# The first two units project 400 tokens before their RMS norms are known, and the norms are multiplied into the results

## The chip, the cores and the metric

The kernel runs on one core of one Trainium2 chip. The time is that of the device, in microseconds (us), from start to end of one execution. The core's engines are TensorE (PE, matrix products into PSUM), VectorE (DVE), ScalarE (ACT), GpSimd (POOL) and SyncE (SP, which issues most DMAs); each works through its own instructions in order.

## The reference, cut to what matters

One encoder layer on two inputs of 256 and 2048 tokens of width 1024, with 16 learned tokens put ahead of each. `w_in` has 2816 columns: attention (q, k, v and a gate) and a convolution part (value, gate, output gate).

```python
def rmsnorm(x, w):
    y = xf * lax.rsqrt(jnp.mean(xf * xf, axis=-1, keepdims=True) + NORM_EPS)
    return y * w
...
    h = rmsnorm(z, norm_w)
    proj = jnp.einsum('bld,de->ble', h, w_in)
    q, k, v, g_att, c_val, c_glu, g_conv = jnp.split(proj, SPLIT_IDX, axis=-1)
...
    u = c_val * jax.nn.sigmoid(c_glu)       # then a convolution of width 31, LayerNorm, SiLU
...
    return z + jnp.einsum('ble,ed->bld', mixed, w_out)
```

The norm of a token is one factor for all of its 1024 values. So `h @ w_in` is the same as `(z * norm_w) @ w_in` times that factor per token.

## The kernel before

All products are made in float32 from two halves: a rounded high half and the low half that is left (`xh` and `xl` of an activation, in groups of up to 400 tokens; `ws` of a weight, both halves in one tile). A product is three matmuls for each 128 rows of depth, in the order (weight high, activation high), (weight high, activation low), (weight low, activation high): `PASSES`. The 1024 rows of depth are 8 steps, so that one half of a unit on one group is 24 matmuls, and an item (unit, group) is 48.

**Units and groups.** A unit is 256 columns of `w_in`: for the first units 128 gate and 128 value columns of the convolution part. The 2320 tokens are in six groups, g0 of 400 columns and g1 to g5 of 384. The order of items begins (unit 0, g0), (unit 1, g0), (unit 0, g1), (unit 1, g1), (unit 0, g2), (unit 1, g2), which are items 0 to 5; item 6 is (unit 2, g0). For an item of the convolution part, `c_group` makes the gate half (`pg`), takes its sigmoid on ACT (`sg`), makes the value half (`pv`), and multiplies both on DVE into `us`, from which DVE later makes the convolution in 30 taps and a first step per tile (L850 and L841).

**What a group needs.** `Prep` prepares a group in steps: `load` brings the transposed tokens in four tiles `xt` (each 2 steps of depth); `first` broadcasts the norms over the partitions by matmuls into `bc` (L661); `scale` multiplies `xt` by weight and norm on DVE (L681); `split` makes `xh` on ACT (L698) and `xl` on DVE and POOL in turn (L707). The norms come from `stats`: the tokens are loaded a second time, with a token in each partition (`xn`, 18 tiles of 128 and one of 16), squared and summed on ACT (L632) and raised to -1/2 on POOL (L122, L123).

**What a unit needs.** `weights` loads a unit in four quarters `wraw` of 256 KB, makes the high half on ACT (L742) and the low half on POOL or DVE (L743).

**The head.** In program order: SP loads `xn0` to `xn3`, `vec` (the norm weight and small vectors), `xt` 0 and 1 of g0, the quarters of unit 0, `xt` 2 and 3, `cw` (the taps), `xn4` to `xn6`, unit 1, then g1. No matmul of a projection starts before the squares of `xn0` to `xn3`, their rstd, the broadcast and the first scale. A scheduler orders the rest; work for later items is put into lists (`later`) that it serves between matmuls (`tick`). After the projections and convolutions, some 560 us in, comes LayerNorm, then attention and the output projection.

Of the kernel before, what the change touches and what calls it, by code (L numbers as in the profile page):

```python
# [75 lines left out]
def hymba_kernel(  # L76
# [56 lines left out]
    def owe(ns):  # L133
        credit[0] -= ns
# [483 lines left out]
    if True:  # L618
# [20 lines left out]
        class Prep:  # L639
# [6 lines left out]
            def load(self, d2):  # L646
# [5 lines left out]
                )  # L652

            def first(self):
                g, n = self.g, self.n
                bc = psum.tile([P, 512], F32, tag="c", name=f"bc{g}")
                segs = [(0, NM, 0)] if g == 0 else []
                for b in range(3 * g, 3 * g + 3):
                    segs.append((blk_local(b)[1], P, b + 1))
                for o, rows, i in segs:  # L660
                    nc.tensor.matmul(  # L661
                        bc[:, o : o + rows],
                        rstd[:rows, i : i + 1].to_broadcast([rows, P]),
                        ident[:rows, :rows],
                        start=True,
                        stop=True,
                    )
                if self.pool:
                    self.bc = sp.tile([P, 400], F32, tag="bcs", name=f"bcs{g}", bufs=1)
                    nc.scalar.copy(self.bc[:, :n], bc[:, :n])  # L670
                else:
                    self.bc = bc

            def scale(self, d2):
# [37 lines left out]
        def weights(k):  # L712

            key = keys[k]
            raw = {}

            def load(eng):
                pool = wl if k % 2 else wr
                ws = pool.tile([P, ND, 2, UW], F32R, tag="ws", name=f"ws{key[0]}_{key[1]}")
                wsplit[key] = ws  # L720
                if key[0] == 1 and key[1] >= CACHE:
                    for q in range(4):
                        part = ws[:, 2 * q : 2 * q + 2].rearrange("p d a n -> p (d a n)")
                        eng.dma_start(part.bitcast(F32), wd[key[1], q])
                    return
                for q in range(4):
                    if k == 1:
                        if q % 2 == 0:
                            pair = cp.tile([P, UWID], F32, tag="us", name=f"wraw{k}_{q}")
                        raw[q] = pair[:, 512 * (q % 2) : 512 * (q % 2) + 512].rearrange("p (a n) -> p a n", n=UW)  # L730
                    else:
                        raw[q] = sp.tile([P, 2, UW], F32, tag="wraw", name=f"wraw{k}_{q}", bufs=4)
                    dma = eng.dma_start(raw[q], w_in[key[1], :, 2 * q : 2 * q + 2, :])
                    if PIN_W <= k < 4:
                        tc.keep_in_program_order(dma)

# [10 lines left out]

            return load, split

# [10 lines left out]
        def proj_et(ws, half_i, g, o=0):  # L760
# [4 lines left out]
            for d in range(ND):  # L765
                for wi, xi in PASSES:
# [39 lines left out]
        def c_group(c, j, ws, g):  # L806
            n = GROUPS[g][1]
            pg = proj_et(ws, 0, g)
            sg = sp.tile([P, 400], F32, tag="sg", name=f"sg{c}_{j}_{g}")
            nc.scalar.activation(sg[:, :n], pg[:, :n], AF.Sigmoid)  # L810
            tick(24 * (n / 2.4 + 3))
            pv = proj_et(ws, 1, g)
            if g == 0:
# [181 lines left out]
        preps[0].load(2)  # L995
        preps[0].load(3)
        nc.sync.dma_start(cw, conv_w)
        nc.vector.scalar_tensor_tensor(kscale, vec[:, 20:21], -(HD ** -0.5), vec[:, 21:22], op0=ALU.mult, op1=ALU.mult)
        for i in (0, 1, 2, 3):
            r[i]()  # L1000
        preps[0].first()
        preps[0].alloc()
        preps[0].scale(0)
        for q in range(4):
            if q < 3:
                preps[0].scale(q + 1)
            preps[0].split(q)
            w01[0][1](q, nc.gpsimd if q % 2 else nc.vector)
        r = {i: stats(i) for i in (4, 5, 6)}
        w01[1][0](nc.sync)  # L1010

        def at_item_start(i, c, u, g):
            if i == 0:
                r[4]()
                r[5]()
                for q in range(4):
                    preps[1].load(q)
                    w01[1][1](q, nc.gpsimd if q % 2 else nc.vector)
                r[6]()
            if i == 1:  # L1020
                later(1, preps[1].first)
                later(1, preps[1].alloc)
                later(1, lambda: preps[1].scale(0))
                for q in range(4):
                    if q < 3:
                        later(1, lambda q=q: preps[1].scale(q + 1))
                    later(1, lambda q=q: preps[1].split(q))
                for k in range(7, 10):
                    later(1, lambda k=k: later(1, stats(k)))
                for q in range(4):  # L1030
                    later(2, lambda q=q: preps[2].load(q))
            if i == I2:
                later(1, preps[2].first)
                later(1, preps[2].alloc)
                later(1, lambda: preps[2].scale(0))
                for q in range(4):
                    if q < 3:
                        later(1, lambda q=q: preps[2].scale(q + 1))
                    later(1, lambda q=q: preps[2].split(q))

# [6 lines left out]

        for i, (c, u, g) in enumerate(items):
            if (c, u) == keys[-1] and g == CHUNKS[c][0]:
                while conv_q[0] or conv_q[1]:  # L1050
# [27 lines left out]
            for k in loads.get(i, []):  # L1078
                load, split = weights(k)
                load(nc.sync)  # L1080
# [85 lines left out]
```

## Time and profile before

| | us |
|---|---|
| time, median of 3 runs | 978.19 |
| the three runs | 978.15, 978.19, 2411.97 |
| the profiled execution, own time | 974.79 |
| its span in the profile | 973.0 |
| PE busy in it | 949.2 (98%), 5740 records |
| DVE busy | 755.9 (78%) |
| ACT busy | 424.6 (44%) |
| POOL busy | 341.2 (35%) |

The span runs from the first to the last instruction of the engines; all times in rows are from its start. Busy shares of several engines overlap. The median is of executions without a profile, so an estimate that is made in the trace has to be carried over by the difference of the two.

### The profile page before, as it was taken

To read this page: it belongs to the slowest core of one execution; us is meant where nothing else is said; L and a number is where in the kernel's file an instruction comes from. 1 tells how busy PE (TensorE), PEld (TensorE's weight loads), DVE (VectorE), ACT (ScalarE), POOL (GpSimd) and SP (SyncE) were. 2 spreads that over 40 slices of the span, in tenths; PEclk is the share of its full clock that TensorE was granted. 3 is DMA by queue.
4 is the path that set the end of the run, shared out by engine and by line. 5 is a ranking of instruction groups with operands and counts; after the bars stand their busy time and mean duration, and the time that the engine had idled before them with its cause. 6 is when DMAs were issued, how large, how long until landed. Compare 5 with 4: busy or idle time off the path is not lost.

```text
span 973.0 us, 16234 instructions
## 1 busy us (share of the span) xinstructions
PE 949.2 (98%) x5740; PEld 890.0 (91%) x5740; DVE 755.9 (78%) x1261; ACT 424.6 (44%) x1156; POOL 341.2 (35%) x541
## 2 busy tenths in 40 slices
PE   5999999999999999999999998899999999999998
PEld 5999999999999999999999998678888888888886
DVE  4759999998987699999993555877776777767772
ACT  6621111343468710111113454766665666666651
POOL 5500000364468300000002464745445544544451
PEclk9999999999999999999999998999999999999999
DMA  9643345785735222233335657954554445544321
GB/s 332 221 181 118 130 170 179 264 286 182 225 124 180 92 73 76 86 128 136 127 135 173 212 141 219 294 171 134 159 177 148 125 152 166 178 127 135 109 88 43
DMA packets 113872, 155.75 MB, mean 160 GB/s; under 512 B 10592, under 2 KB 77296, under 8 KB 113792
## 3 DMA queue, kind: packets, MB, share of 16 engines
q1 hardware_dynamic: 113648, 154.11, 48.1%
q0 software_dynamic: 144, 0.62, 0.4%
q8 instruction: 45, 0.74, 0.3%
q14 instruction: 35, 0.29, 0.1%
HBM read 101.00 MB, written 54.31 MB: 160 GB/s over the span
## 4 chain that ended last, share of the span: by engine, by line
PE 91%; DMA 3%; DVE 2%; POOL 1%; issue 1%; SPq 1%; ACT 0%; POOLq 0%; DVEq 0%
PE pj L767 42%; PE y L538 20%; PE pj L783 13%; PE O L464 5%; PE pT L429 4%; PE S L316 4%; DMA woraw<-in_w_out 2%; DMA snk<-in_sink 1%; DMA wraw<-in_w_in 1%; PE O L316 1%; PE lnt L183 1%; PE qT L316 1%; PE lnu L202 1%; PE kt L941 0%; PE pT_m L426 0%
## 5 line engine op out<-in xcount | busy, mean ns | idle before, releaser
L767 PE MATMUL pj<-xh,ws 128*128 128x384 f32 (+1 forms) x1536 | 397.2, 339 | 2.5 <-ACT xh L698 2.5
L850 DVE SCALAR_TENSOR_TENSOR y<-us,cw,y 128x1167 f32<-128x1167 f32 x240 | 329.0, 1428 | 0.6
L767 PEld LDWEIGHTS pj<-xh,ws 128*128 128x128 f32 x1536 | 282.3, 189 | 2.8 <-ACT xh L698 2.8
L767 PE MATMUL pj<-xl,ws 128*128 128x384 f32 (+1 forms) x768 | 262.5, 342 | 0.1
L783 PE MATMUL pj<-ws,xh 128*128 128x256 f32 (+1 forms) x880 | 165.8, 286 | 0.0
L767 PEld LDWEIGHTS pj<-xl,ws 128*128 128x128 f32 x768 | 144.7, 188 | 1.1 <-POOL xl L707 0.7
L783 PEld LDWEIGHTS pj<-ws,xh 128*128 128x128 f32 (+1 forms) x880 | 137.8, 189 | 0.3
L783 PE MATMUL pj<-ws,xl 128*128 128x256 f32 (+1 forms) x440 | 125.4, 285 | 0.0
L383 ACT ACTIVATE sb<-sb,nm 128x304 f32<-128x304 f32 (+4 forms) x144 | 77.1, 535 | 45.3 <-DVE nm L371 43.7
L538 PE MATMUL y<-wo,mch 128*128 128x512 f32 x288 | 95.9, 414 | 0.0
L538 PE MATMUL y<-wo,mah 128*128 128x512 f32 x288 | 93.7, 406 | 0.0
L441 DVE TENSOR_TENSOR pl<-pT,ph 128x512 fp32r<-128x512 f32 x100 | 69.0, 690 | 29.0 <-ACT ph L440 28.5
L875 ACT ACTIVATE go<-pj 128x384 f32<-128x384 f32 x48 | 23.6, 491 | 154.5 <-PE pj L767 145.3
L371 DVE CUSTOM_DVE_ANT_0 sb<-S,bias,nsnk 128x304 f32<-128x304 f32 (+4 forms) x144 | 73.5, 511 | 15.0 <-PE S L316 14.5
L783 PEld LDWEIGHTS pj<-ws,xl 128*128 128x128 f32 (+1 forms) x440 | 83.2, 189 | 0.2
L122 POOL TENSOR_SCALAR ssk<-ssk 128x2 f32<-128x2 f32 x18 | 6.4, 356 | 213.0 <-ACT sqk L889 212.9
L440 ACT CAST ph<-pT 128x512 fp32r<-128x512 f32 x100 | 58.2, 583 | 40.2 <-PE pT L429 39.5
L406 POOL TENSOR_SCALAR sb<-sb,es 128x304 f32<-128x304 f32 (+4 forms) x144 | 72.8, 525 | 3.6
L316 PEld LDWEIGHTS S<-kw,q 128*128 128x128 f32 x288 | 53.8, 191 | 17.9 <-DVE nm L371 5.9
L122 POOL TENSOR_SCALAR ssq<-ssq 128x4 f32<-128x4 f32 (+2 forms) x55 | 28.3, 515 | 114.4 <-ACT xn L632 76.9
L316 PE MATMUL S<-kw,q 128*128 128x304 f32 (+4 forms) x288 | 62.6, 299 | 5.3 <-DVE nm L371 5.3
L429 PE MATMUL pT<-ident,sb 128*128 128x128 f32 x400 | 61.6, 274 | 1.3 <-POOL sb L406 1.0
(118 smaller groups left out, 1441.8 us busy)
## 6 DMA issues: line engine op xcount, KB each, us to landing
wd<-ws SPq DMA_DIRECT2D x36, 512.0 KB, 5.7
ws<-wd SPq DMA_DIRECT2D x36, 512.0 KB, 5.3
wraw<-in_w_in SPq DMA_DIRECT2D x52, 256.0 KB, 5.6
xn<-in_z SPq DMA_DIRECT2D x18, 512.0 KB, 5.7
gd<-go SPq DMA_DIRECT2D x48, 192.0 KB, 2.1
yo<-in_z SPq DMA_DIRECT2D x36, 256.0 KB, 2.6
out_y<-yo SPq DMA_DIRECT2D x36, 256.0 KB, 2.4
kw<-kd SPq DMA_DIRECT2D x16, 512.0 KB, 5.7
```

Source lines behind the costliest of these rows:

```text
L316: r = f(*a, **k)
L371: nc.vector.tensor_tensor_reduce(out=sb[:, n, c0:c1], in0=ps[:, 0:w], in1=cst["bias"][:, kv, n, c0 - QB * n : c1 - QB * n], scale=1.0, sca ...
L383: nc.scalar.activation(sb[:, n, c0:c1], sb[:, n, c0:c1], AF.Exp, bias=nm[:, n : n + 1], scale=-1.0, accum_out=rs[:, n : n + 1],)
L406: nc.gpsimd.tensor_scalar(sb[:, k, a0:a1], sb[:, k, a0:a1], es[:, k : k + 1], 1.0, op0=ALU.mult, op1=ALU.mult)
L429: nc.tensor.transpose(pt[:, hl, :], sbt[b, kv][:, hl, KCOL[k] : KCOL[k] + P], ident)
L440: nc.scalar.copy(ph, pt)
L441: nc.vector.tensor_tensor(pl, pt, ph, op=ALU.subtract)
L464: nc.tensor.matmul(o, lhs, t, start=(start and i == 0), stop=(stop and i == 1))
L538: nc.tensor.matmul(ps, mh[mi][:, e % 4, :], wo[e, wi][:, cols], start=(e == 4 and k == 0), stop=(e == 3 and k == 2),)
L767: nc.tensor.matmul(ps[:, :n], ws[:, d, wi, P * half_i : P * half_i + P], x[xi][:, d, o : o + n], start=(k == 0), stop=(k == 3 * ND - 1),)
L783: nc.tensor.matmul(ps[:rows, :UW], x[xi][:, d, o : o + rows], ws[:, d, wi, :], start=(k == 0), stop=(k == 3 * ND - 1),)
L850: nc.vector.scalar_tensor_tensor(y[:, yo + o0 : yo + o1], u[:, o0 + k : o1 + k], cw[:, j, k : k + 1], y[:, yo + o0 : yo + o1], op0=ALU.mul ...
```

## The change

In the head, all five engines now follow the program's order, written out by hand (`MAN0`), up to the end of item 2's matmuls. For g0 no norm is known when the first two units begin: `plain` makes `xh` as the tokens times the norm weight (ACT) and `xl` as what that leaves (DVE, one scalar_tensor_tensor). The four tiles `xt` are then squared in place (POOL two, ACT two, 800 columns each), added up by DVE to one tile of 128 x 400, and summed over the partitions by four matmuls with a column of ones, which stand after the first quarter of unit 1. From this come the rstd of g0; the broadcasts of g0 and g1 stand after the third quarter of unit 1. `c_gate` and `c_value` multiply the results by the broadcast (`bcs`, a copy in SBUF). For the later units g0 is loaded again and prepared as before (`scale` and `split`, in the lists of items 4 and 5). `xn0` to `xn3` and their squares are gone. `proj_pair` makes both halves of an item at once, quarter by quarter of the depth. Fourteen matmuls of the identity by itself (`heat`) stand ahead of the first product. SP's order is now `xt` and weight quarter in turn for unit 0 and g0, unit 1, `xn4` to `xn6`, g1, `cw`, and so on; `vec` is the first DMA of ACT's queue.

```diff
+MAN0 = {getattr(mybir.EngineType, e) for e in ("Activation", "DVE", "Pool", "PE", "SP")}
...
+            def plain(self, d2):
+                n, xt = self.n, self.xt[d2]
+                xh, xl = xg[self.g]
+                for d in (2 * d2, 2 * d2 + 1):
+                    nc.scalar.mul(xh[:, d, :n], xt[:, d % 2, :n], nw[:, d : d + 1])
+                for d in (2 * d2, 2 * d2 + 1):
+                    nc.vector.scalar_tensor_tensor(
+                        xl[:, d, :n], xt[:, d % 2, :n], nw[:, d : d + 1], xh[:, d, :n], op0=ALU.mult, op1=ALU.subtract
+                    )
+            def square(self, d2, eng):
+                a = self.xt[d2][:, :, : self.n]
+                if eng is nc.scalar:
+                    nc.scalar.activation(a, a, AF.Square)
+                else:
+                    eng.tensor_tensor(a, a, a, op=ALU.mult)
...
+            def sums(self):
+                n, a = self.n, self.xt[3]
+                nc.vector.tensor_tensor(a[:, 0, :n], a[:, 0, :n], a[:, 1, :n], op=ALU.add)
+                ps = psum.tile([P, 512], F32, tag="d", name="ssq0")
+                for o, rows, i in self.segments():
+                    nc.tensor.matmul(ps[:rows, i : i + 1], a[:, 0, o : o + rows], ones, start=True, stop=True)
+                for rows, c0, c1 in ((P, 1, 4), (NM, 0, 1)):
+                    dst = rstd[:rows, c0:c1]
+                    nc.vector.tensor_scalar(dst, ps[:rows, c0:c1], 1.0 / D, EPS, op0=ALU.mult, op1=ALU.add)
+                    nc.gpsimd.tensor_tensor(dst, dst, half[:rows, 0 : c1 - c0], op=ALU.pow)
...
+        def c_gate(c, j, g, pg, bc=None):
...
+                nc.vector.tensor_tensor(sg[:, :n], pg[:, :n], bc[:, :n], op=ALU.mult)
+                nc.scalar.activation(sg[:, :n], sg[:, :n], AF.Sigmoid)
...
+        def c_value(c, j, g, pv, sg, bc=None):
+            if bc is not None:
+                nc.vector.tensor_tensor(sg[:, :n], sg[:, :n], bc[:, :n], op=ALU.mult)
...
-        r = {i: stats(i) for i in (0, 1, 2, 3)}
-        nc.sync.dma_start(vec, vecs)
-        preps[0].load(0)
-        preps[0].load(1)
-        w01[0][0](nc.sync)
...
+        man.enter_context(tc.manual_schedule(engines=MAN0))
+        nc.scalar.dma_start(vec, vecs)
+        for q in range(4):
+            p0.load(q)
+            w01[0][3](q, nc.sync)
+        w01[1][0](nc.sync)
+        r = {i: stats(i) for i in (4, 5, 6)}
+        for _ in range(HEAT):
+            nc.tensor.matmul(heat[:, :P], ident, ident, start=True, stop=True)
+        def feed(q):
+            p0.plain(q)
+            w01[0][1](q, nc.vector if q % 2 else nc.gpsimd)
+            if q == 1:
+                p0.square(0, nc.gpsimd)
+            if q == 2:
+                p0.square(1, nc.scalar)
+            if q == 3:
+                p0.square(2, nc.gpsimd)
+                p0.square(3, nc.scalar)
+        feed(0)
+        ps0 = proj_pair(wsplit[keys[0]], 0, lambda q: feed(q + 1) if q < 3 else None)
+        p0.add(1, 0)
+        w01[1][1](0, nc.vector)
+        for q in range(1, 4):
+            w01[1][1](q, nc.gpsimd)
+        p0.add(3, 2)
+        p0.add(3, 1)
+        def between(q):
+            if q == 0:
+                p0.sums()
+                for i in (4, 5, 6):
+                    r[i]()
+            if q == 2:
+                p0.first()
+                p1.first()
+        ps1 = proj_pair(wsplit[keys[1]], 0, between)
+        nc.scalar.copy(bc0[:, : p0.n], p0.bc[:, : p0.n])
+        sg0 = c_gate(0, 0, 0, ps0[0], bc0)
+        p1.scale(0)
+        p1.split(0)
+        c_value(0, 0, 0, ps0[1], sg0, bc0)
...
+        ps2 = proj_pair(wsplit[keys[0]], 1)
+        man.close()
...
+            if i == 4:
+                    later(1, lambda q=q: p0.load(q))
+                later(2, p0.first)
...
+            if i < 3:
+                continue
```

The pieces below are what each engine's list of instructions holds; numbers behind a tile's name count the tiles. First DVE in the head of before, from its first scale on: g0's four tiles are xt_0_116, xt_1_118 (and 2, 3), the weights of unit 0 are ws_0_120.

```order
L681 SCALAR_TENSOR_TENSOR xt_0_116<-xt_0_116,vec,bc_151 128x400 x2
L681 SCALAR_TENSOR_TENSOR xt_1_118<-xt_1_118,vec,bc_151 128x400 x2
L743 TENSOR_TENSOR ws_0_120<-wraw_0_121,ws_0_120 128x2x256
L707 TENSOR_TENSOR xl_157<-xt_0_116,xh_156 128x400
L707 TENSOR_TENSOR xl_157<-xt_1_118,xh_156 128x400
L743 TENSOR_TENSOR ws_0_120<-wraw_2_125,ws_0_120 128x2x256
```

DVE at the same place now, from its first instruction on data to the last addition ahead of the sums; ws_1_129 is unit 1.

```order
L686 SCALAR_TENSOR_TENSOR xl_158<-xt_0_113,vec,xh_157 128x400 x2
L686 SCALAR_TENSOR_TENSOR xl_158<-xt_1_117,vec,xh_157 128x400 x2
L788 TENSOR_TENSOR ws_0_112<-wraw_1_119,ws_0_112 128x2x256
L686 SCALAR_TENSOR_TENSOR xl_158<-xt_2_121,vec,xh_157 128x400 x2
L686 SCALAR_TENSOR_TENSOR xl_158<-xt_3_125,vec,xh_157 128x400 x2
L788 TENSOR_TENSOR ws_0_112<-wraw_3_127,ws_0_112 128x2x256
L1098 SCALAR_TENSOR_TENSOR kscale<-vec 128x1
L699 TENSOR_TENSOR xt_1_117<-xt_1_117,xt_0_113 128x800
L788 TENSOR_TENSOR ws_1_129<-wraw_0_130,ws_1_129 128x2x256
L699 TENSOR_TENSOR xt_3_125<-xt_3_125,xt_2_121 128x800
L699 TENSOR_TENSOR xt_3_125<-xt_3_125,xt_1_117 128x800
L704 TENSOR_TENSOR xt_3_125<-xt_3_125 128x400
```

The scales are gone from here, all eight low halves of g0 are DVE's, and four additions have come in, with unit 1's first low half between them. POOL in the head of before, after the rstd of the first token tiles:

```order
L743 TENSOR_TENSOR ws_0_120<-wraw_1_123,ws_0_120 128x2x256
L707 TENSOR_TENSOR xl_157<-xt_0_116,xh_156 128x400
L707 TENSOR_TENSOR xl_157<-xt_1_118,xh_156 128x400
L743 TENSOR_TENSOR ws_0_120<-wraw_3_127,ws_0_120 128x2x256
L707 TENSOR_TENSOR xl_157<-xt_2_129,xh_156 128x400
```

POOL now, up to the tiles `us` of the first two units:

```order
L788 TENSOR_TENSOR ws_0_112<-wraw_0_115,ws_0_112 128x2x256
L695 TENSOR_TENSOR xt_0_113<-xt_0_113 128x800
L788 TENSOR_TENSOR ws_0_112<-wraw_2_123,ws_0_112 128x2x256
L695 TENSOR_TENSOR xt_2_121<-xt_2_121 128x800
L788 TENSOR_TENSOR ws_1_129<-wraw_0_130,ws_1_129 128x2x256
L788 TENSOR_TENSOR ws_1_129<-wraw_2_133,ws_1_129 128x2x256 x2
L865 MEMSET us_0_249 128x15
```

POOL has no low half of an activation any more, five of weights (the third has a quarter of the pair tile that begins with wraw_0_130) and two squares. PE now, where the first quarter of unit 1 ends (pj_262 is its gate half, pj_263 its value half):

```order
L831 MATMUL pj_263<-xl_158,ws_1_129 128x400
L831 MATMUL pj_263<-xh_157,ws_1_129 128x400
L707 MATMUL ssq_277<-ones,xt_3_125 16x1
L707 MATMUL ssq_277<-ones,xt_3_125 128x1 x3
L831 MATMUL pj_262<-xh_157,ws_1_129 128x400
L831 MATMUL pj_262<-xl_158,ws_1_129 128x400
```

The four sums stand in PE's list behind 60 projection matmuls and ahead of 36; before, the first norms' broadcast was PE's first instruction.

## Rows read from the trace of the kernel before

**Rows 1.** The page, the chain that ended last, by engine.

```profile
PE 91%; DMA 3%; DVE 2%; POOL 1%; issue 1%; SPq 1%; ACT 0%; POOLq 0%; DVEq 0%
```

**Rows 2.** Chain of waits, first 120 us: start, us, what.

```profile
4.63 7.93 DMA wraw<-in_w_in
...
15.01 1.40 POOL xl L707
...
24.82 0.44 PE bc L661 x4
...
39.28 80.82 PE pj L767 x456
```

**Rows 3.** Timeline of PE: start, us, engine, line, instruction, [idle before].

```profile
13.00 1.04 PE L767 MATMUL pj<-xh,ws 128*128 128x400 f32 x2 [2.46 <-ACT xh L698]
...
18.65 0.54 PE L767 MATMUL pj<-xh,ws 128*128 128x400 f32 x2
19.02 0.34 PE L767 MATMUL pj<-xl,ws 128*128 128x400 f32 x1
...
68.66 0.35 PE L767 MATMUL pj<-xl,ws 128*128 128x400 f32 x1
```

**Rows 4.** Timelines of DVE and POOL, 13 to 25 us.

```profile
13.35 0.57 DVE L707 TENSOR_TENSOR xl<-xt,xh 128x400 fp32r<-128x400 f32 x1
15.42 1.53 DVE L743 TENSOR_TENSOR ws<-wraw,ws 128x512 fp32r<-128x512 f32 x1
24.29 0.69 DVE L743 TENSOR_TENSOR ws<-wraw,ws 128x512 fp32r<-128x512 f32 x1 [0.35 <-ACT ws L742]
...
13.54 1.52 POOL L743 TENSOR_TENSOR ws<-wraw,ws 128x512 fp32r<-128x512 f32 x1 [3.86 <-ACT ws L742]
17.82 1.29 POOL L743 TENSOR_TENSOR ws<-wraw,ws 128x512 fp32r<-128x512 f32 x1
21.60 1.06 POOL L707 TENSOR_TENSOR xl<-xt,xh 128x400 fp32r<-128x400 f32 x1
```

**Rows 5.** Timeline of POOL beside the taps; last, the taps' line with durations in ns (min/median/max).

```profile
60.94 0.21 POOL L865 COPY carry<-us 128x30 f32<-128x30 f32 x1 [15.42 <-DVE us L822]
69.37 1.35 POOL L865 COPY carry<-us 128x30 f32<-128x30 f32 x1 [8.22 <-DVE us L822]
...
186.11 8.32 POOL L122 TENSOR_SCALAR ssq<-ssq 128x1 f32<-128x1 f32 x1 [64.11 <-ACT xn L632]
...
L850 DVE SCALAR_TENSOR_TENSOR y<-us,cw,y x240: 1412/1427/1440, 62.9 to 521.8; 128x1167 f32<-128x1167 f32 x120
```

**Rows 6.** Groups by shape: busy us, mean ns of one, idle before.

```profile
L742 ACT CAST ws<-wraw 128x512 fp32r<-128x512 f32 x52 | 29.1, 618 | 19.8 <-PE pj L767 14.8 <-DMA wraw<-in_w_in 5.0
L681 DVE SCALAR_TENSOR_TENSOR xt<-xt,vec,bc 128x400 f32<-128x400 f32 x8 | 4.5, 623 | 2.5 <-PE bc L661 2.5
L707 DVE TENSOR_TENSOR xl<-xt,xh 128x400 fp32r<-128x400 f32 x4 | 3.6, 926 | 0.4 <-ACT xh L698 0.4
```

**Rows 7.** ACT's timeline at the first squares; DMA rate from 7 to 15 us, 40 slices.

```profile
5.00 1.06 ACT L632 ACTIVATE xn<-xn 128x1024 f32<-128x1024 f32 x1 [0.85 <-DMA xn<-in_z]
...
6.30 1.06 ACT L632 ACTIVATE xn<-xn 128x1024 f32<-128x1024 f32 x1 [0.15 <-DMA xn<-in_z]
...
GB/s 390 400 400 392 384 392 376 392 389 390 267 266 195 102 113 102 154 133 256 348 358 420 369 440 362 454 362 426 384 407 380 415 392 376 370 390 372 388 365 433
```

**Rows 8.** Stretches: us, busy PE, PEld, DVE, ACT, POOL (instructions), granted clock, DMA share, GB/s.

```profile
10.00:18.00 8.00, 5.41 (x15) 4.08 (x16) 6.99 (x11) 4.36 (x9) 4.46 (x4) 1.00 1.03 375
...
50.00:60.00 10.00, 10.00 (x58) 10.00 (x58) 0.56 (x1) 0.49 (x1) 0.00 (x0) 1.00 0.12 45
...
599.50:605.40 5.90, 5.90 (x28) 5.90 (x29) 5.08 (x16) 4.44 (x13) 4.39 (x7) 0.51 0.67 217
605.70:612.00 6.30, 6.30 (x56) 6.30 (x55) 4.91 (x15) 4.69 (x14) 2.84 (x6) 1.00 0.75 202
```

**Rows 9.** Timeline of PE at the start of the stretch with the lower clock.

```profile
599.44 0.73 PE L316 MATMUL S<-kw,q 128*128 128x176 f32 x2 [3.42 <-DVE nm L371]
```

More of the change, by code (lines that the diff above doesn't have):

```diff
@@ L715, in weights, with tile, part @@
             raw = {}
[L717 to L725 removed]
+            def tile():
+                pool = wl if k % 2 else wr
+                wsplit[key] = pool.tile([P, ND, 2, UW], F32R, tag="ws", name=f"ws{key[0]}_{key[1]}")
+            def part(q, eng):
+                if k == 1:
+                    if q % 2 == 0:
+                        raw["pair"] = cp.tile([P, UWID], F32, tag="us", name=f"wraw{k}_{q}")
+                    o = 512 * (q % 2)
+                    raw[q] = raw["pair"][:, o : o + 512].rearrange("p (a n) -> p a n", n=UW)
+                else:
+                    raw[q] = sp.tile([P, 2, UW], F32, tag="wraw", name=f"wraw{k}_{q}", bufs=4)
+                dma = eng.dma_start(raw[q], w_in[key[1], :, 2 * q : 2 * q + 2, :])
+                if PIN_W <= k < 4:
+                    tc.keep_in_program_order(dma)
+            def load(eng):
+                tile()
+                ws = wsplit[key]
                 for q in range(4):
[L727 to L730, printed above, removed]
[L731 to L735 removed]
+                    if key[0] == 1 and key[1] >= CACHE:
+                        flat = ws[:, 2 * q : 2 * q + 2].rearrange("p d a n -> p (d a n)")
+                        eng.dma_start(flat.bitcast(F32), wd[key[1], q])
+                    else:
+                        part(q, eng)
             def split(q, eng):
@@ L746, in split @@
                     later(1, lambda: nc.sync.dma_start(wd[key[1], q], part.bitcast(F32)))
-            return load, split
+            return load, split, tile, part
         pj_n = [0]
@@ L774, in proj_et, with proj_pair @@
                     k += 1
+            return ps
+        def proj_pair(ws, g, between=lambda q: None):
+            n = GROUPS[g][1]
+            x = xg[g]
+            ps = [pj(), pj()]
+            for q in range(4):
+                for half_i in range(2):
+                    for d in (2 * q, 2 * q + 1):
+                        for i, (wi, xi) in enumerate(PASSES):
+                            nc.tensor.matmul(
+                                ps[half_i][:, :n],
+                                ws[:, d, wi, P * half_i : P * half_i + P],
+                                x[xi][:, d, :n],
+                                start=(d == 0 and i == 0),
+                                stop=(d == ND - 1 and i == 2),
+                            )
+                between(q)
             return ps
@@ L1002, in hymba_kernel @@
[L1002 to L1010, printed above, removed]
-        def at_item_start(i, c, u, g):
[L1013 to L1023, printed above, removed]
+        man = ExitStack()
@@ new lines, in hymba_kernel @@
+        p0.add(1, 0)
[4 more added lines that the diff above has]
+        p0.add(3, 1)
+        u_tiles(0, 0)
+        u_tiles(0, 1)
+        for q in range(4):
+            p1.load(q)
+        nc.sync.dma_start(cw, conv_w)
+        def between(q):
[6 more added lines that the diff above has]
+                p1.first()
@@ new lines, in hymba_kernel @@
+        ps1 = proj_pair(wsplit[keys[1]], 0, between)
+        p1.alloc()
+        bc0 = sp.tile([P, D], F32, tag="xn", name="bcs")
+        nc.scalar.copy(bc0[:, : p0.n], p0.bc[:, : p0.n])
[3 more added lines that the diff above has]
+        c_value(0, 0, 0, ps0[1], sg0, bc0)
+        sg1 = c_gate(0, 1, 0, ps1[0], bc0)
+        p1.scale(1)
+        p1.split(1)
+        c_value(0, 1, 0, ps1[1], sg1, bc0)
+        for q in (2, 3):
+            p1.scale(q)
+            p1.split(q)
@@ L1024, in at_item_start @@
+        ps2 = proj_pair(wsplit[keys[0]], 1)
+        man.close()
+        r = {i: stats(i) for i in (7, 8, 9)}
+        c_value(0, 0, 1, ps2[1], c_gate(0, 0, 1, ps2[0]))
+        for q in range(4):
+            p2.load(q)
+        for i in (7, 8, 9):
+            r[i]()
+        p2.first()
+        p2.alloc()
+        def at_item_start(i, c, u, g):
+            if i in (3, 5):
+                p = p2 if i == 3 else p0
+                later(1, lambda: p.scale(0))
                 for q in range(4):
@@ L1025, in at_item_start @@
                     if q < 3:
[L1026 to L1029, printed above, removed]
+                        later(1, lambda q=q: p.scale(q + 1))
+                    later(1, lambda q=q: p.split(q))
+            if i == 4:
                 for q in range(4):
[L1031 to L1039, printed above, removed]
+                    later(1, lambda q=q: p0.load(q))
+                later(2, p0.first)
@@ L1078, in hymba_kernel @@
             for k in loads.get(i, []):
-                load, split = weights(k)
+                load, split = weights(k)[:2]
                 load(nc.sync)
```

40 lines of the change are left out of this document (27 added, 13 removed).

## The prediction

> **What bounds the kernel now.** I read the page's chain of what ended last first: TensorE (PE) carries 91% of the span and DMA 3% [rows 1]. So a change of the head can gain or lose only what it moves the point from which PE runs without a gap. The chain of the first 120 us shows that point: a weight load until 12.56, then GpSimd's (POOL's) low half of an activation at 15.01, and from 16.46 nothing but PE, in which the last piece is 456 matmuls in 80.82 us, 0.177 us each, and a norm broadcast costs 0.22 (x4 in that row are two broadcasts) [rows 2]. In PE's timeline the first projection matmul is at 13.00, after a wait; from 18.65 two follow each other in 0.37 us, 0.185 each for 400 columns. Item 6, the first product of unit 2, starts 0.18 before the 68.66 row, at 68.5 [rows 3]. From there to the stage change after the convolution I treat the program as the same before and after, so **the shift of item 6's first matmul is the shift of the end**.
>
> **The two engines that feed PE.** The timelines of VectorE (DVE) and POOL show something the page does not: they take turns. A weight low half on POOL takes 1.29 us alone, but 1.52 when DVE is in a subtract that ends at 13.92. DVE's low half takes 0.69 alone, but 1.53 from 15.42: it ends at 16.95, and POOL's subtract had the time until 16.41 [rows 2, 4]. So whoever is second waits, then needs 0.54 of 0.69: about 0.15 of each instruction lies under its predecessor.
>
> **The change part by part.**
>
> *Earlier start.* The squares of token rows and their loads leave the path. ACT squares the first 128 rows at 5.00, when 64 + 512 KB have landed, and the next 1.30 later, so 512 KB take 1.3 us (394 KB/us) [rows 7]. Now 400 KB of columns come first: about 4.6. The first weight quarter, 256 KB, is there 0.65 later, 5.2. The DMA slices from 9 us show what the first weights did: nine slices of 0.2 us at 102 to 267 GB/s instead of 390, which is 1.0 us lost [rows 7]. I add it: 6.2. Bounds 0 and 1.0, since the order of weights and columns is another. Then the cast (0.62 [rows 6]) and POOL's low half (1.29): PE's third matmul, which needs it, at 8.2. PE is then 5 us earlier than before.
>
> *PE's new work before item 6.* Four sums of squares by matmul, bounded by 0 and a broadcast each (0.22): 0.8 at most, which I take. Broadcasts: 6 were in the run up to item 6, now 14, 8 × 0.22 = 1.8. The 14 warming matmuls come before the data: like a broadcast each, 3.1, or 6.2 at the lower clock; started before 2.0 they end before 8.2 in both cases. They are free.
>
> *What DVE and POOL now do before the sums of squares.* POOL: five weight low halves at 1.29 and two squares of 800 columns. The slope from 400 columns (1.06) to 512 (1.29) [rows 4] gives 1.9 (bounds 1.29 and 2.12). Sum 10.3. DVE: eight activation low halves (L686); the nearest row is the scale with the same operation and 400 columns, 0.62 [rows 6]; three weight low halves, 2.1; three additions of 800 columns and one of 400. From 0.57 (400) and 0.69 (512) [rows 4] the slope gives 1.0 each, 3.6. Sum 10.6. Beside each other this would be 10.6; **in turns** it is 20.9 less 22 × 0.15, 17.6.
>
> Does L686 take turns as well? It is a scalar_tensor_tensor, not a subtract of two tensors, but reads xt and xh, both in SBUF. The rows on the convolution taps (L850, the same operation with us and y in SBUF) speak both ways. Their 240 durations lie between 1412 and 1440 ns, so nothing on POOL delays them. But a POOL copy of 30 columns took 1.35 us there, and one POOL instruction on a single column 8.32 us, in a stretch of taps [rows 5]: POOL is kept out by them. I take it that L686 takes turns.
>
> The Trainium skill has a rule for this ("SBUF — State Buffer", section "Who interferes with whom"): DVE and GpSimd share a pair of ports, as an exclusive lock for the whole instruction; DVE with at most one SBUF input goes free, with two it contends. The subtracts' rows agree, and the scale L681, whose third input is in PSUM, would be the free kind. By that rule L686 is locked and the sum below stays as it is; without it, it is the first rival's.
>
> *The sums of squares.* The first two L686 run from 5.2 to 6.2 with POOL idle; from 6.9 (cast done) the other 16.6 us run in turns: 23.5. ACT's squares cost waits of about 0.5: 24.0. PE could have been there after 58 matmuls from the third, 8.2 + 58 × 0.185 = 18.9. So **PE waits 5.1 us**, spread over unit 0 and the first quarter of unit 1. Then 0.8 for the sums, 36 matmuls (6.7) and 7 broadcasts (1.5): unit 1 is done at 33.0.
>
> *Items 2 to 5.* 192 × 0.177 = 34.0 and 7 broadcasts 1.5: 68.5. Group 1's first activation comes late: its broadcast ends at 30.7, then the copy to SBUF (some 0.5), one gate multiply (0.6), two scales (1.2) and a cast (0.5): 33.5, 0.5 after PE. The next quarters need two scales, a gate or value multiply and a subtract of 1.06 on POOL beside 2.2 us of matmuls, about even; I allow 1.0. 70.0.
>
> *The clock.* In the head of before the granted clock is 1.00 of full speed (2.4 GHz) from 10 to 18 us, in spite of PE's waits. Later, after an idle 3.42 us, it is 0.51 (1.2 GHz) for 5.9 us: 28 matmuls there, 56 in the 6.3 us after it [rows 8, 9], so 28 × (0.211 - 0.113) = 2.8 lost. The changed head has waits of one or two microseconds each; bounds 0 and 2.8, I take 1.0. **Item 6 starts at 71.0 instead of 68.5: +2.5.**
>
> *What the later normalisation of group 0 costs.* It is loaded again (1.6 MB), scaled (8 × 0.62) and split (4 × 0.93 on DVE [rows 6]), 8.7 us of DVE and four broadcasts, counted above. From 50 to 60 us of before DVE is busy 0.56 of 10 us, POOL not at all, DMA 0.12 [rows 8]. So DVE and the loads have room, and it is hidden; without that cover it would cost item 6 up to 8.7. The statistics of token tiles 4 to 6 stay on ACT and POOL. ACT has 16 casts of at most 0.62 and two squares of at most 1.06 before the sums [rows 6, 7], 12 us of the 24. SP's queue now issues the columns and weights of units 0 and 1 ahead of those token tiles; nobody waits for them before the broadcasts of group 1, at 29.
>
> **Sum.** Span and what lies around it: the profiled execution took 974.79, the median of the timed runs is 978.19. With +2.5 the profile would be 977.3 and the time **980.7**, 0.3% slower; a measurement here tells about 2% from no change.
>
> **The rivals.**
>
> *A: L686 goes beside POOL.* For it: the uniform tap rows [rows 5]. Then the turns lose 8 × (0.62 - 0.15) = 3.8, PE waits 1.3 instead of 5.1, and with no long wait the clock term goes too (1.0): item 6 at 66.1, **975.8**, faster than before. The sign flips where PE's waits before the sums fall from 5.1 below 2.6. If no two of these instructions ever take turns, another 1.6 goes (the waits left and the allowances): 974.2.
>
> *B: the clock falls and stays low.* PE runs unit 0 in short pieces between waits. If it gets 1.2 GHz until unit 1 is fed, as after the 3.42 us [rows 8, 9], 2.8 instead of 1.0 are lost, and about the same once more for a second such stretch or a longer chain of waits (the first cast late, POOL's low halves last in turn): item 6 at about 74, **984**. Against it: the head of before kept 1.00.
>
> *C: the shift does not arrive at the end.* DMA has 3% of the chain, 29 us, of which the head is 8 [rows 1, 2]; the other 21 are loads in the stage change, and if these were issued regardless of PE, they would take up 2.5 us: **978.2**. Against it: SP's queue is one list in program order, with stores that wait for PE and DVE ahead of those loads, so they move along.
>
> *D: over 2% slower*, by one mechanism: the manual order of all engines makes one of them wait for another that stands behind it, as where the second pass over group 0 meets weights of unit 2 on DVE; it decides from 20 us, which is twice the whole second pass. I see no such pair.
>
> **How the numbers follow.** Chances: the forecast (977.9 to 983) 0.50, A 0.28, B 0.14, C 0.07, D 0.01. Eight in ten lie from 974.0 (A with its lower end) to 984.5 (B). The likeliest case alone has 977.9 to 983, and its ends are the bounds of the slow first weights (-1.0), the clock (-1.0 to +1.8) and half a microsecond each of squares and allowances. Faster by over 2% (below 958.6) would need more than the whole head gives up: 0.01; slower by over 2% (above 997.8): 0.02.
>
> **What the profile after would show.** Third matmul of unit 0 at about 8.2; the L686 rows between 0.6 and over 1.5 us, each ending some 0.5 after a POOL end (if all are 0.6 beside busy POOL, A holds); the sum-of-squares matmuls at 24; unit 1 done at 33; 128x400 matmuls of unit 2 first at 71.0; a granted clock in the first 24 us between 0.5 and 1. PE without a gap from there to the stage change, and L746's subtracts over before unit 2. Wrong it would be by a first weight at under 5.5 or over 7.5, by ssq before 21, or by a gap ahead of unit 2.

## The result, and the profile after

| | median us | runs | ratio to the kernel before, 95% interval |
|---|---|---|---|
| kernel before | 978.15 | 9 | |
| changed kernel | 980.29 | 9 | 1.0027 [1.0018, 1.0036] |
| changed kernel, second batch | 979.63 | 11 | 1.0031 [1.0020, 1.0043] |

The change makes the kernel 0.3% slower, some 2.5 to 3 us. (In the later batches the kernel before had 977.2 to 977.3 as median of 21 to 35 runs.) One run of the kernel before, of 2411.97, is left out of the ratio. The profiled execution took 981.13 with a span of 979.4.

In what follows L831 and L812 are projection matmuls, L684 and L686 the high and low halves of g0's tokens, L787 and L788 those of weights, L695 and L693 the squares on POOL and ACT, L699 and L704 the additions, L707 (with `ssq`) the sums and L666 the broadcasts. The timeline of PE after the change, from the warming matmuls to the broadcasts and then at the start of unit 2 (start, us, instruction, [idle before <- releaser]):

```profile
1.36 5.57 PE L1081 MATMUL heat<-ident 128*128 128x128 f32 x28 [1.36 <-POOL ident masks.py:199]
6.68 0.43 PE L831 MATMUL pj<-xh,ws 128*128 128x400 f32 x1
...
8.03 0.63 PE L831 MATMUL pj<-xh,ws 128*128 128x400 f32 x2 [0.73 <-POOL ws L788]
...
10.95 0.64 PE L831 MATMUL pj<-xh,ws 128*128 128x400 f32 x2 [0.46 <-DVE ws L788]
...
16.08 0.63 PE L831 MATMUL pj<-xh,ws 128*128 128x400 f32 x2 [0.47 <-DVE ws L788]
...
20.01 0.34 PE L831 MATMUL pj<-xh,ws 128*128 128x400 f32 x1
23.21 1.58 PE L707 MATMUL ssq<-ones,xt 128*16 128x1 f32 x8 [2.86 <-DVE xt L704]
24.66 0.68 PE L831 MATMUL pj<-xh,ws 128*128 128x400 f32 x1
...
26.14 0.54 PE L831 MATMUL pj<-xl,ws 128*128 128x400 f32 x1
26.47 0.87 PE L831 MATMUL pj<-xh,ws 128*128 128x400 f32 x2
27.14 0.54 PE L831 MATMUL pj<-xl,ws 128*128 128x400 f32 x1
...
31.56 1.92 PE L666 MATMUL bc<-ident,rstd 16*128 16x16 f32 x14
...
35.65 0.44 PE L831 MATMUL pj<-xh,ws 128*128 128x384 f32 x1
...
72.28 0.52 PE L812 MATMUL pj<-xh,ws 128*128 128x384 f32 x2
72.64 0.35 PE L812 MATMUL pj<-xl,ws 128*128 128x400 f32 x1
```

The third projection matmul starts at 8.03; before it started at 13.97, behind the two of the first row of [rows 3]. Then come three waits for low halves, 0.73, 0.46 and 0.47, and one of 2.86 for the additions on DVE. Behind the sums three matmuls take 1.0 us (26.14 to 27.14) instead of 0.55. Item 2 starts at 35.65. Item 6 starts 0.18 ahead of the 72.64 row, at 72.5, against 68.5 before [rows 3]. Stretches of the same trace (busy us of PE, PEld, DVE, ACT, POOL, then the granted clock, DMA share and GB/s) show the reason for the slow matmuls:

```profile
1.40:6.60 5.20, 5.20 (x27) 5.20 (x28) 1.18 (x2) 3.02 (x5) 0.00 (x0) 1.00 0.86 232
...
20.30:23.20 2.90, 0.06 (x1) 0.00 (x0) 2.83 (x2) 1.24 (x4) 2.61 (x6) 0.97 0.64 155
24.70:29.60 4.90, 4.90 (x16) 4.85 (x17) 0.21 (x2) 0.00 (x0) 3.63 (x8) 0.50 0.62 193
```

After 2.9 us without work PE has 0.50 of full speed (1.2 GHz) in the 4.9 us behind the sums, as behind the 3.42 of [rows 8, 9]. DVE and POOL in the stretch that PE waits for (their timelines):

```profile
5.08 1.18 DVE L686 SCALAR_TENSOR_TENSOR xl<-xt,vec,xh 128x400 fp32r<-128x400 f32 x2 [4.19 <-ACT xh L684]
...
16.01 0.98 DVE L699 TENSOR_TENSOR xt<-xt,xt 128x800 f32<-128x800 f32 x1
...
17.52 4.09 DVE L699 TENSOR_TENSOR xt<-xt,xt 128x800 f32<-128x800 f32 x2
21.64 1.52 DVE L704 TENSOR_TENSOR xt<-xt 128x400 f32<-128x400 f32 x1
...
7.93 1.93 POOL L695 TENSOR_TENSOR xt<-xt 128x800 f32<-128x800 f32 x1
...
13.14 1.85 POOL L695 TENSOR_TENSOR xt<-xt 128x800 f32<-128x800 f32 x1 [1.06 <-DVE xl L686]
17.44 5.29 POOL L788 TENSOR_TENSOR ws<-wraw,ws 128x512 fp32r<-128x512 f32 x3 [2.45 <-ACT ws L787]
```

The first addition, alone, takes 0.98. The next two take 4.09 together beside three low halves of unit 1 on POOL, which take 5.29 instead of 3 × 1.29 [rows 4]; the last addition, 400 columns, takes 1.52. And in the chain of waits two of the low halves L686 appear where POOL makes a square or a low half (start, us, what):

```profile
10.82 1.78 DVE xl L686 x2
...
13.53 1.89 DVE xl L686
...
17.59 2.02 DVE xt L699
...
19.64 1.98 DVE xt L699
```

The chain goes on with the last addition to the sums. The L686 that begins at 13.53 lasts until 15.42, 0.43 behind the end of POOL's square (13.14 + 1.85 = 14.99); alone one takes 0.59 (the two at 5.08). So these instructions exclude each other, as the subtracts of [rows 4] do.

### The profile page after: what moved, and what is told of

The parts are those of the page before. It is cut to its first block, busy times and chain, and to the rows that moved or that the text cites. A ratio compares the mean times of both kernels' runs of the same rounds, so it can differ in the third digit from the quotient of the medians.

```text
span 979.4 us, 16356 instructions
## 1 busy us (share of the span) xinstructions
PE 958.6 (98%) x5784; PEld 898.9 (92%) x5784; DVE 770.1 (79%) x1279; ACT 426.0 (44%) x1159; POOL 345.3 (35%) x538
## 4 chain that ended last, share of the span: by engine, by line
PE 88%; DMA 4%; DVE 4%; POOL 1%; issue 1%; ACT 1%; SPq 1%; POOLq 0%; DVEq 0%
PE pj L812 39%; PE y L542 20%; PE pj L847 12%; PE O L468 4%; PE pT L433 4%; PE S L320 3%; DMA woraw<-in_w_out 2%; PE pj L831 2%; DMA xt<-in_zt 1%; DMA snk<-in_sink 1%; PE O L320 1%; PE lnt L187 1%; PE qT L320 1%; PE lnu L206 1%; PE bc L666 0%
## 5 line engine op out<-in xcount | busy, mean ns | idle before, releaser
L812 PE MATMUL pj<-xh,ws 128*128 128x384 f32 (+1 forms) x1440 | 371.6, 338 | 0.0
L812 PEld LDWEIGHTS pj<-xh,ws 128*128 128x128 f32 x1440 | 262.6, 188 | 0.0
L812 PE MATMUL pj<-xl,ws 128*128 128x384 f32 (+1 forms) x720 | 244.3, 339 | 0.0
L812 PEld LDWEIGHTS pj<-xl,ws 128*128 128x128 f32 x720 | 135.2, 188 | 0.0
L445 DVE TENSOR_TENSOR pl<-pT,ph 128x512 fp32r<-128x512 f32 x100 | 69.0, 690 | 29.6 <-ACT ph L444 29.1
L509 POOL TENSOR_TENSOR at<-at,ga 128x256 f32<-128x256 f32 x36 | 26.9, 747 | 104.8 <-DVE at L503 104.8
L126 POOL TENSOR_SCALAR ssq<-ssq 128x4 f32<-128x4 f32 (+1 forms) x51 | 25.3, 496 | 107.9 <-ACT xn L636 68.8
```

Of the source, the lines that this page charges most:

```text
L445: nc.vector.tensor_tensor(pl, pt, ph, op=ALU.subtract)
L812: nc.tensor.matmul(ps[:, :n], ws[:, d, wi, P * half_i : P * half_i + P], x[xi][:, d, o : o + n], start=(k == 0), stop=(k == 3 * ND - 1),)
```

## The experiments

The theory after the result: DVE and POOL take turns, this delays the sums of squares, PE idles 2.9 us before them, and its clock falls behind that. Rival 1: the sums follow the landing of columns and ACT's casts, not the turns. Rival 2: the low clock has another cause than the wait. Rival 3: the second pass over group 0 costs the time.

| run | sums start | PE's wait there | from sums to broadcasts | item 6 | median us | ratio, 95% interval |
|---|---|---|---|---|---|---|
| changed kernel | 23.2 | 2.9 | 8.4 | 72.5 | 980.29 | 1.0027 [1.0018, 1.0036] |
| e1, squares to ACT | 22.6 | 3.3 | 6.9 | 70.4 | 979.57 | 1.0022 [1.0011, 1.0033] |
| e2, low halves later | 21.6 | 0.9 | 5.4 | 67.8 | 976.02 | 0.9985 [0.9973, 0.9996] |
| e3, both | 21.2 | 1.6 | 5.4 | 67.5 | 975.74 | 0.9986 [0.9973, 0.9998] |
| e4, no warming | 23.5 | 2.6 | 6.9 | 71.4 | 979.28 | 1.0015 [1.0004, 1.0026] |
| e5, sums later | 21.3 | none | | 65.3 | 973.81 | 0.9963 [0.9950, 0.9976] |
| e6, no second pass | 23.7 | 2.9 | 8.5 | 72.1 | 979.33 | 1.0021 [1.0012, 1.0030] |
| e7, wait filled | 23.7 | 0.2 | 5.4 | 70.0 | 977.90 | 1.0002 [0.9994, 1.0011] |
| e8, before, warmed at the start | | | | 73.3 | 982.02 | 1.0045 [1.0033, 1.0057] |
| e9, before, warmed later | | | | 68.7 | 978.60 | 1.0009 [0.9999, 1.0018] |
| kernel before, second trace | | | | 69.7 | | |

From the sums to the broadcasts PE has the same work in the changed kernel and its variants, but for e5: four sums and 24 matmuls. From the broadcasts to item 6 they all take 40.9 us, but for e6. So item 6 moves with the start of the sums and with this stretch.

**e1: the two squares of POOL to ACT**

```diff
-            if q == 1:
-                p0.square(0, nc.gpsimd)
...
             if q == 3:
-                p0.square(2, nc.gpsimd)
+                p0.square(0, nc.scalar)
+                p0.square(2, nc.scalar)
                 p0.square(3, nc.scalar)
```

> The two squares that POOL makes go to ACT. Theory (DVE and POOL take turns, and this makes the sums late): the low halves L686 beside the squares shrink from 1.2 to 1.9 us to 0.6, the sums start near 20.5 instead of 23.2, PE waits 0.3 instead of 2.9, and the stretch at 0.50 of the clock behind that wait is gone (2.4 us): item 6 near 67.5 instead of 72.5, time 975 to 977. Rival 1 (the sums follow the landing of the columns and ACT's casts): sums at 23 as now, 980. Rival 2 (the low clock comes from the start and not from the wait): sums near 20.5, but still 0.50 for some 5 us: item 6 near 70, 978.

DVE's timeline of e1:

```profile
8.26 1.18 DVE L686 SCALAR_TENSOR_TENSOR xl<-xt,vec,xh 128x400 fp32r<-128x400 f32 x2 [1.99 <-ACT xh L684]
...
14.25 0.99 DVE L699 TENSOR_TENSOR xt<-xt,xt 128x800 f32<-128x800 f32 x1
16.28 0.69 DVE L788 TENSOR_TENSOR ws<-wraw,ws 128x512 fp32r<-128x512 f32 x1 [1.04 <-ACT ws L787]
16.89 4.08 DVE L699 TENSOR_TENSOR xt<-xt,xt 128x800 f32<-128x800 f32 x2
21.01 1.52 DVE L704 TENSOR_TENSOR xt<-xt 128x400 f32<-128x400 f32 x1
```

PE's timeline and a stretch of e1:

```profile
22.58 0.96 PE L707 MATMUL ssq<-ones,xt 128*16 128x1 f32 x8 [3.26 <-DVE xt L704]
...
29.50 1.93 PE L666 MATMUL bc<-ident,rstd 16*128 16x16 f32 x14
```

```profile
23.90:27.00 3.10, 3.10 (x11) 3.07 (x10) 0.00 (x0) 0.00 (x0) 2.76 (x6) 0.50 0.77 222
```

The turns of L686 are gone as expected: every pair takes 1.18, and the first addition starts at 14.25 instead of 16.01. But the sums gain only 0.6. Of the 1.8 gained DVE gives 1.04 back, waiting for ACT's cast for unit 1, which now stands behind three squares, and the additions take 4.08 beside POOL's low halves as before. I expected 2.7 and had not followed ACT's queue. PE comes earlier (it no longer waits for DVE's low halves in unit 0), idles longer, 3.3, and its clock falls to 0.50 again. But the low clock costs less than in the changed kernel: the sums still take 0.96, the slow matmuls end at 27.0, and the stretch from the sums to the broadcasts is 1.4 us shorter. These 1.4 and the 0.6 are the 2.1 us by which item 6 comes earlier. This confirms the lock on L686 and shows that the squares alone don't decide.

**e2: unit 1's third and fourth low half to DVE, behind the sums**

```diff
-        for q in range(1, 4):
-            w01[1][1](q, nc.gpsimd)
+        w01[1][1](1, nc.gpsimd)
...
-        u_tiles(0, 0)
-        u_tiles(0, 1)
...
                 p0.sums()
+                for p in (2, 3):
+                    w01[1][1](p, nc.vector)
...
+                u_tiles(0, 0)
+                u_tiles(0, 1)
```

(`u_tiles` holds POOL's four MEMSETs of `us`, 0.24 us together.)

> The low halves of unit 1's third and fourth quarter go from POOL, beside the additions, to DVE behind the sums. Theory of turns: two of the three POOL instructions between 17.4 and 22.7 are gone, each worth 1.29 less 0.15: sums near 21, PE waits under 1, no low clock: item 6 near 68, 976. Rival 1 (landings and casts): sums at 23, 980. Rival 2: the low halves are now late for PE's third quarter of unit 1: a new wait of 1 to 2 us there, 978 to 980.

DVE's timeline of e2, the same additions:

```profile
17.77 3.12 DVE L699 TENSOR_TENSOR xt<-xt,xt 128x800 f32<-128x800 f32 x2
20.92 0.57 DVE L704 TENSOR_TENSOR xt<-xt 128x400 f32<-128x400 f32 x1
```

3.12 + 0.57 instead of 4.09 + 1.52: 1.9 us less (2.3 expected), with nothing changed in what DVE does until there. PE's wait is 0.9, no matmul behind the sums is slow, and item 6 comes 4.6 us earlier. This decides against rival 1: DVE's landings and casts are as they were. The new wait for the moved low halves, which I had named as a rival, isn't there. The changed kernel with this edit is some 1 us faster than the kernel before.

**e3: e1 and e2 together**

> Both of the edits before. Theory of turns: PE is the later one at the sums, which start near 19.8 without a wait: item 6 near 67, time 975, hardly less than with either alone (the two gains do not add). Rival 1: as the changed kernel, 980. If the gains add, 972, the waits were not the same ones.

The gains don't add: item 6 at 67.5, 0.3 us ahead of e2. PE came 1.0 us earlier to the sums (19.3 + one matmul) and waited 1.6; the sums at 21.2 and not at 19.8, since DVE's wait for ACT remained.

**e4: without the warming matmuls** (`HEAT`, and its PSUM tile)

> The 14 warming matmuls are gone. Theory: the matmuls of unit 0 then run 0.33 us apart up to some 12 us, as those of the kernel before from 13.0 to 18.4, which costs PE 2.2 us before the sums, but the sums wait for DVE until 23.2 in any case: PE's wait shrinks from 2.9 to under 1 and the low clock behind it goes: item 6 near 70, 978. Rival (the warming is worth what it gives in unit 0): item 6 2.2 later than now, 982.5.

PE's timeline and two stretches of e4:

```profile
10.27 0.54 PE L831 MATMUL pj<-xl,ws 128*128 128x400 f32 x1
10.60 0.87 PE L831 MATMUL pj<-xh,ws 128*128 128x400 f32 x2
11.27 0.54 PE L831 MATMUL pj<-xl,ws 128*128 128x400 f32 x1
```

```profile
8.40:11.60 3.20, 3.17 (x10) 3.14 (x10) 3.20 (x4) 2.88 (x6) 2.17 (x2) 1.00 1.06 397
...
26.00:29.00 3.00, 3.00 (x10) 2.97 (x10) 0.00 (x0) 0.00 (x0) 2.39 (x7) 0.50 0.86 291
```

The start is at half rate as expected (three matmuls in 1.0 us up to 11.6; the 1.00 in that row doesn't tell it). But PE came to the sums only 0.5 us later than with warming, since the slow matmuls took the place of the waits for low halves, so it still idled 2.6 and the clock still fell to 0.50. The theory's first half is right, its consequence (wait under 1) wrong. Item 6 is 1.1 earlier than with warming although the sums start 0.3 later: as in e1 the low clock sets in behind the sums, and from the sums to the broadcasts PE takes 6.9 us and not 8.4. Why it set in later in e1 and e4, with waits of 3.3 and 2.6 on both sides of the 2.9, no run here shows. The time is 1.0 lower with overlapping intervals: **in this kernel the warming buys nothing that the time shows**.

**e7: the wait filled with work**

```diff
+                for _ in range(12):
+                    nc.tensor.matmul(ps[:, 128:256], ident, ident, start=True, stop=True)
                 for o, rows, i in self.segments():
```

> Twelve more matmuls of the identity stand on PE ahead of the sums of squares, 12 x 0.22 = 2.6 us of work in the wait of 2.9. Theory (the half rate from 24.7 to 29.5 follows from PE's idle time): the matmuls behind the sums run 0.18 apart, the four sums take 1.0 instead of 1.6, and item 6 comes at 69.5 to 70, time 978, though work was added. Rival (the half rate has another cause, or the added matmuls delay the sums): item 6 at 72.5 or later, 980 or more.

PE's timeline and a stretch of e7:

```profile
20.69 2.84 PE L708 MATMUL ssq<-ident 128*128 128x128 f32 x24
23.71 0.96 PE L710 MATMUL ssq<-ones,xt 128*16 128x1 f32 x8 [0.18 <-DVE xt L705]
...
29.10 1.93 PE L667 MATMUL bc<-ident,rstd 16*128 16x16 f32 x14
```

```profile
24.70:28.80 4.10, 4.10 (x23) 4.09 (x23) 0.21 (x2) 0.00 (x0) 3.34 (x8) 1.00 0.73 223
```

The sums come 0.5 us later than in the changed kernel, yet item 6 is 2.5 earlier and the time 2.4 lower, with 12 matmuls more. The clock is 1.00 where it was 0.50, and the four sums take 0.96 instead of 1.58. From the sums to the broadcasts PE takes 5.4 us instead of 8.4, as in e2 and e3. So without the idle time before the sums the low clock doesn't come (against rival 2), and it cost the changed kernel 3.0 us, of which the later sums take 0.5 back here. The length of the wait alone doesn't set this cost: behind the 3.3 of e1 and the 2.6 of e4 it is 1.5, behind the 0.9 of e2 and the 1.6 of e3 nothing.

**e6: no second pass over group 0** (the lists of items 4 and 5 lose its load, broadcast, scale and split)

> The changed kernel without the second loading, scaling and splitting of group 0 (left out: the later units then use group 0 without its norms). Theory (the second pass is hidden but for its four broadcasts and the change of PE's order around them): item 6 near 71.2 instead of 72.5, time 979. Rival (DVE, POOL or DMA time of the second pass comes back later, in the convolution that DVE bounds there): 8.7 us of DVE less, time 972 to 976, with item 6 hardly earlier.

Item 6 at 72.1 though the sums were 0.5 later: from the broadcasts to item 6 it takes 40.0 and not 40.9, so the pass costs the PE time of its four broadcasts and no more. The time is 979.33, within the interval of the changed kernel. Rival 3 falls, also for the convolution: with some 8 us of DVE less up to 560 us, the time from item 6 to the end stays within the scatter of the other traces (below).

**e8 and e9: the kernel before, with warming**

At the start (e8), and behind the norms' broadcast and dependent on the last norm (e9):

```diff
+        for _ in range(30):
+            nc.tensor.matmul(heat[:, :P], ident, ident, start=True, stop=True)
...
+        for _ in range(8):
+            nc.tensor.matmul(heat[:, :P], rstd[:, 3:4].to_broadcast([P, P]), ident, start=True, stop=True)
```

> The kernel before with 30 matmuls of the identity at PE's start. Theory (the matmuls 0.33 us apart from 13 to 18.4 are PE at half rate after an idle start): they run 0.18 apart, but PE waits for low halves until 16.5 in any case, so that only the six or so matmuls behind that gain, 0.9 us, item 6 at 67.6, 976.5. Rival (the half rate there is DVE's and POOL's pace and not the clock): nothing changes, item 6 at 68.5, 977.

> The kernel before with eight more matmuls like the norms' broadcast behind it on PE (10.5 to some 13 us), the other engines' order in the head being that of the kernel before. Theory (PE is at half rate from 13 to 18.4 because it comes out of an idle start): the matmuls behind the wait of 16.5 run 0.18 apart, item 6 at 67.5 to 68, time 976.5. Rival (the pace there is DVE's and POOL's): nothing changes, item 6 at 68.5, 977.

e8 doesn't test it: with the matmuls in its list the scheduler put ACT's and DVE's weight work ahead of the activations, and the first product came at 15.96 instead of 13.00. PE had then idled 4.30 and idled 2.28 once more, and its granted clock was 0.51 from 19 to 23 us, the warming notwithstanding. In e9 the order stayed. Its PE timeline:

```profile
10.08 3.62 PE L1004 MATMUL heat<-ident,rstd 128*128 128x128 f32 x16
...
15.93 0.53 PE L767 MATMUL pj<-xh,ws 128*128 128x400 f32 x2
16.29 0.35 PE L767 MATMUL pj<-xl,ws 128*128 128x400 f32 x1
...
20.81 0.45 PE L767 MATMUL pj<-xl,ws 128*128 128x400 f32 x1 [1.07 <-DVE xl L707]
```

The matmuls are 0.18 apart where they were 0.33, so that was the clock after an idle start; but then PE waits 1.07 for a low half, and item 6 is at 68.7. The kernel before is held by DVE and POOL at the same place, and time saved on PE is lost to them.

**e5: a version that beats both.** e3, and: the additions follow the squares at once, unit 1's first cast stands ahead of ACT's last two squares, POOL does the statistics of token tiles 4 to 6 first, and the sums stand one quarter later:

```diff
-            if q == 0:
-                p0.sums()
+            if q == 1:
                 for i in (4, 5, 6):
                     r[i]()
+                p0.sums()
+                w01[1][1](3, nc.vector)
...
```

> The version with ACT's four squares and the late low halves, and in addition: the sums stand behind unit 1's second quarter (not the first), the additions follow the squares at once, POOL does the statistics of token tiles 4 to 6 ahead of the power for group 0. Theory (a wait of PE for the sums, and the clock behind it, are all that the head loses): DVE's additions end near 20.5, PE comes to the sums near 21.5, no wait and no stretch at half rate: item 6 near 64.5 instead of 67.5, time 973, 0.4 to 0.5% under the kernel before. Rival: the wait moves to the norms' broadcast, which now has only one quarter (2.2 us) between sums and broadcast: 1 to 2 us of PE there and the clock with it, item 6 near 67, 975.5.

PE's timeline of e5:

```profile
20.97 0.35 PE L834 MATMUL pj<-xh,ws 128*128 128x400 f32 x1
21.25 0.96 PE L710 MATMUL ssq<-ones,xt 128*16 128x1 f32 x8
...
24.15 0.34 PE L834 MATMUL pj<-xh,ws 128*128 128x400 f32 x1
24.43 1.92 PE L666 MATMUL bc<-ident,rstd 16*128 16x16 f32 x14
```

No wait at the sums, none at the broadcasts, no slow stretch; item 6 at 65.3, 973.81 us: 0.4% faster than the kernel before, 0.7% than the changed one. So the idea itself (start without the norms) gains 3 to 4 us at the head (against 68.5 and 69.7 in the two traces of before) once the sums don't hold PE.

**Second traces of both kernels**

> The changed kernel once more, unedited, for a second trace and more timed runs. If the head's shift (item 6 at 72.5 against 68.5) arrives whole at the end, the time is 4 us over the kernel before; if the stage change takes some of it up, 2.5 us as in the first runs. The stretch from item 6 to the end differed by 2.4 us between traces so far; a second trace shows how much of that is scatter.

> The kernel before once more, unedited, for a second trace: item 6 at 68.5 within 0.5, and from item 6 to the end between 904.5 and 907 us, if that stretch scatters for both kernels alike.

The changed kernel has item 6 at 72.5 again. The kernel before has it at 69.7 in its second trace, because PE waits for the first low half until 14.84 and runs at half rate to 20.3 (before: 13.97 and 18.4). So the trace from which I predicted was one of its short ones (974.79, below the median of 977 to 978), and the shift of the head is 2.8 to 4.0. From item 6 to the end of the span the thirteen traces have 904.5 (before) to 908.8 (e9), with before's two at 904.5 and 907.3 and the changed kernel's at 906.9 and 906.1: scatter of the rest of the program, for both alike. The times of the eight changed variants follow item 6 almost one to one, from 65.3 and 973.81 to 72.5 and 980.29 (6.5 us of time on 7.1, by the rows 65.52 and 72.64).

## Why the prediction was right

The time (980.29 against 980.7) and the mechanism came out; the terms not all, and part of the match is luck. The sums' start was taken 0.8 too late and the stretch behind it, to the start of item 2, 2.4 too short (12.4 against 10.0 with the clock's 1.0), so item 6 came 1.5 later than predicted. But the head of the trace that I started from was short by 1.2 us against the second one, and the two nearly cancel. Its 974.79 also lay 3.4 under the median, which I carried over as if it belonged to the profile. The profiled executions of the changed kernel took 981.13 and 980.38, not 977.3, and lie by their own medians.

- **Start.** Third matmul at 8.2 predicted, 8.03 and 8.25 in the two traces. Right, the slow first weights included.
- **Turns.** Additions of 1.0 (0.98 alone), squares of 1.9 (1.93, 1.85) and L686 locked against POOL: right. The sums could start at 23.2, predicted 24.0. PE's waits were 0.73 + 0.46 + 0.47 + 2.86 = 4.5, predicted 5.1. Rival A falls with the L686 of 1.89 us beside a square and 0.59 in e1, where POOL is free. The rule in the Trainium skill ("SBUF — State Buffer", "Who interferes with whom"), that a DVE instruction with two SBUF inputs and a GpSimd one that reads SBUF exclude each other, agrees with it. The taps' even durations, which spoke for A, don't speak against the lock: beside them POOL has only instructions on 30 columns or fewer (its low halves of 288 to 322 us come behind the taps of that stretch), and these are the ones that wait. One on a single column takes 0.19 us where DVE is free and 0.91 among the taps (the kernel before):

  ```profile
  195.14 0.19 POOL L122 TENSOR_SCALAR ssq<-ssq 128x1 f32<-128x1 f32 x1
  206.72 0.91 POOL L122 TENSOR_SCALAR ssq<-ssq 128x1 f32<-128x1 f32 x1
  200.76 18.92 DVE L850 SCALAR_TENSOR_TENSOR y<-us,cw,y 128x1167 f32<-128x1167 f32 x14
  ```
- **The sums** were mis-sized: 1.58, where 0.8 was called the most. At full clock they take 0.96 (e2, e3, e5, e7), at the lower one 1.58.
- **The clock** was mis-sized: 1.0 allowed, measured 3.0 together with the sums' 0.6 (8.4 against 5.4 us from the sums to the broadcasts, e7 against the changed kernel). I took a value between the bounds because the head of before showed 1.00 "in spite of PE's waits"; e4 and e9 show that PE was at half rate there all the same, while that column read 1.00. The row was no evidence for a clock that holds (the last section says why).
- **Items 2 to 5**: 35.5 and 1.5 allowed, 37.0; measured 72.5 - 35.65 = 36.8. Right. The second pass is hidden (e6).
- **Item 6** was 72.5, not 71.0: 1.5 too early by the clock and the sums, and unit 1 was done at about 35.6, not 33.0. The base, 68.5, was a short head; the second trace has 69.7. Against that one, the shift is 2.8. This is why +2.5 fits the timed difference of 2 to 3 although the head of the trace moved by 4.0.
- **Rival B** happened in its first part (0.50 in the 4.9 us behind the sums) and not in its second. **Rival C** isn't seen: variants that differ by 7.1 at item 6 differ by 6.5 in time.
- **What can be told apart** was put at about 2%; the intervals here are ±0.1%, so 0.3% is a difference.

## What to carry to other kernels

An earlier start is worth what the latest of the engines that feed PE leaves of it: count the instructions of DVE and POOL in turns, not beside each other, wherever both read two operands from SBUF as here, and keep POOL's off the stretch on which PE's next wait depends (two low halves moved by some microseconds gave 4 us here). A wait of PE can cost more than itself: behind waits of 2.6 to 3.3 us the low clock took another 1.5 to 3 us here, behind 0.9 and 1.6 nothing. Another quarter of work ahead of a sum (e5), or even useless matmuls (e7), were cheaper than the wait. And take two traces of the kernel before: its head alone differed by 1.2 us, half of the effect.

## What the runs showed that I had not expected

- The granted clock reads 1.00 in stretches in which PE comes from an idle start and issues a 400-column matmul every 0.33 us (e4, 8.4 to 11.6 us: 10 matmuls in 3.2), but 0.50 behind a wait later on (24.7 to 29.6) with the same spacing. The reason is in the traces' own clock records: the first begins at 18.2 us in the kernel before, 12.0 in e4 and 15.5 in e9, with 1.00 each time, and from there the matmuls are 0.18 apart. Ahead of it there is no record, and the column shows 1.00 without one. So the 1.00 of [rows 8] from 10 to 18 us says nothing of the clock; the spacing of the matmuls tells the pace.
- The power for the norms on POOL (L711) took 0.87 us where DVE was idle, and 1.90 in e2 and e3 beside two low halves on DVE: in the turns, an instruction on three columns costs what stands ahead of it.
